# A hybrid attention and convolution step: four convolution inputs as filling of the attention, and two gates by Strassen's product

## The chip, the cores and the metric

The kernel runs on one core of one Trainium2 chip. The metric is the device time of one execution in microseconds. A core has a matrix engine (PE, with its weight loads shown as PEld), a vector engine (DVE), a scalar engine (ACT), a general engine (POOL) and queues that issue transfers (SP's above all). Matrix products go to PSUM, eight banks of 512 float32 columns for each of 128 partitions; everything else lives in SBUF.

## What is computed

One step of an encoder for 1024 frames of a new stream and 32 frames of a running one (TT = 1056 columns in all, D = 1024 channels). Cut to what matters:

```python
h = rmsnorm(x, norm_g)
q, k = rmsnorm(h @ Wq) / 8, rmsnorm(h @ Wk)       # per head of 64, 16 heads
v, logf = h @ Wv, log_sigmoid(h @ Wf + b_f)
ga, gb, ma, mb = h @ Wga, h @ Wgb, h @ Wma, h @ Wmb
u = (h @ Wua) * sigmoid(h @ Wub)                  # the conv input
o = softmax(q k^T + C[t] - C[s], causal) v        # C = cumsum(logf)
conv = causal depthwise conv of u, width 31
ya = (o * silu(ga)) @ w_pa
yb = (silu(layernorm(conv)) * silu(gb)) @ w_pb
y = x + (sigmoid(ma) * ya + sigmoid(mb) * yb) @ w_out
```

Outputs are y, k, v, logf and the last 30 rows of u.

## The kernel before

Data stand with channels on partitions. The normed input is held as two tiles, xh (rounded to the fast matmul type) and xl (the remainder), 8 channel tiles (kt) by 1056 columns each. Each weight block of 1024 x 128 is loaded as raw, split into wh (ACT, `split_w`, L91) and wl (POOL, L94), and a product is wh·xh + wl·xh + wh·xl: three matmuls for each kt.

`steps` (L144) projects one block of 128 output channels: three column ranges of 352, each with 8 kt, so 24 steps of three matmuls (L102). After each step `beat` (L118) is called. It runs what was put off with `later` for that count of beats, adds `pace["rate"]` to a credit, and while the credit is not negative it takes small work for DVE from two lists, `chores` and `taps`, and subtracts its cost (1.0 for a tap, 0.1 for the first tap of a tile, which ACT does).

`taps` holds the depthwise convolution: for each of 8 channel tiles 31 taps (`conv_taps`, L254; L264 is one multiply-add over 1086 columns on DVE), then two entries of `sums` (L251) that add the result to the mean and the sum of squares for the layernorm. A tile's taps enter when both of its projections "ub" and "ua" are done (`u_done`, L292). `u_tile` pumps taps beyond 66 at once; `pump` ignores the credit.

The order is: input and first tile u0; u1, values, u2, values, u3; k and q for eight pairs of heads with u4, u5, u6 between; u7; eight "ga" gates with Silu on ACT; the attention; two last gates; then the projections "pa", "pb" and "out". Up to the attention the orders of PE, DVE and ACT are the program's own (`manual_schedule`); from there on only PE's is, and a scheduler places the others.

The attention (L997 on) walks 132 items: 16 heads of 8 query blocks, and 4 items for the running stream. A block's scores go to PSUM (L938), DVE takes the maximum (L943), ACT the exponential (L946), POOL scales (L949), PE transposes (L966), ACT and DVE split the result (L970, L971), PE multiplies by the values (L982, L983). Scores are started three items ahead. After each item four steps of `filler` run: 22 gates of gb, ma and mb (`gate_steps`, L765), evacuated by ACT from one PSUM bank (pool pq) and stored in scratch. The layernorm's statistics also run there. In the head's last part, DVE multiplies the output with Silu(ga) (L993).

Behind it `a_half` (L1110) splits the attention's output for "pa"; `ln_out` (L1119) makes the other branch's input during "pa"; `outproj` (L1147) runs each projection, its first block with kt outermost.

Of the kernel before, what the change touches and what calls it, by code (L numbers as in the profile page):

```python
# [8 lines left out]
F32 = mybir.dt.float32  # L9
# [19 lines left out]
LNO = ((0,), (1, 2), (3,), (4, 5), (6,), (7,), ())  # L29
LNEXP = "natural_log_exp_and_others"  # L30
NFILL = 22
R_U, R_V, R_QK, R_G, R_A = 0.25, 0.17, 0.19, 0.27, 0.12
# [16 lines left out]
def build(tc, xT, xt, wv, wf, ckT, cv, clT, stT, vec, cst, yT, kT, vO, lfO, cpT, csT):  # L49
# [26 lines left out]
    rawp = [wp]  # L76

# [10 lines left out]
    def split_w(raw, offset=2000):  # L88
        with tc.high_priority(offset=offset):
            wh = wp.tile([128, KT, 128], F32R, name="wh", tag="wh")  # L90
            nc.scalar.copy(wh, raw)  # L91
            wl = wp.tile([128, KT, 128], F32R, name="wl", tag="wl")
            for k0, k1 in WSP:
                nc.gpsimd.tensor_sub(wl[:, k0:k1, :], raw[:, k0:k1, :], f32(wh[:, k0:k1, :]))  # L94
        return wh, wl
# [40 lines left out]
    def fetch():  # L136

        if plan:
            key = plan.pop(0)
            if not plan:  # L140
                rawp[:] = [wp]
# [28 lines left out]
    sg = pool("sg")  # L170

    def t352(name, bufs):
        return sg.tile([128, CH], F32, name=name, tag=name, bufs=bufs)

    pq = pool("pq", 1, space=PS)
    pps = ExitStack()
    pjA = pool("pjA", 4, stack=pps, space=PS)
# [15 lines left out]
    cvp = pool("cvp", 2, stack=pcv)  # L193
    us = {}
    taps = []
    cvt = [cvp]
# [57 lines left out]
    def conv_taps(f):  # L254
        u = us.pop(f)

        def tap(i):
            w = vec_t[:, V_WDW + f * KC + i:V_WDW + f * KC + i + 1]
            if i == 0:
                y = sides["y", f] = cvt[0].tile([128, CW], F32, name="y", tag="y")  # L260
# [4 lines left out]
            if f == 7:  # L265
                tc.keep_in_program_order(t)
# [3 lines left out]
        items = [lambda i=i: tap(i) for i in range(KC)]  # L270
        if f == 7:
            taps.extend(pend + items)
            pend.clear()
        else:
            taps.extend(items[:4] + pend + items[4:])
            pend[:] = sums(f) if f else []
# [7 lines left out]
    def u_tile(f):  # L284
        if f > 2:
            pump(len(taps) - 66)
        u = us[f] = cvt[0].tile([128, UW], F32, name="u", tag="u", bufs=3 if f < 7 else 1)
# [10 lines left out]
    def u_steps(f, pj):  # L298
# [13 lines left out]
        for g, ev in (("ub", ev_ub), ("ua", ev_ua)):  # L312
# [172 lines left out]
    for f in range(8):  # L485
        if f in (2, 4, 6):
            plan.extend([("ub", 3 + f // 2), ("ua", 3 + f // 2)])
        plan.extend([("k", f), ("q", f)])
    plan.extend([("ub", 7), ("ua", 7)] + [("ga", f) for f in range(8)] + [("gb", 0)])
# [24 lines left out]
    rxs = [pool(f"rx{i}", 1, stack=prw) for i in range(2)]  # L514
    rawp.extend(rxs)
# [3 lines left out]
    p2 = ExitStack()  # L519
    u7p = pool("u7p", 1, stack=p2, side="right")  # L520
    pv = ExitStack()
    zp = pool("zp", 1, stack=pv, side="right")
# [4 lines left out]
    xsm = vp.tile([128, KT, TS], F32, name="xsm", bufs=1)  # L527
    nc.vector.tensor_add(xsm, f32(xh[:, :, T:]), f32(xl[:, :, T:]))

    def split_v(c):  # L530
        wh2, wl2, raws2 = [], [], []
        for hf in range(2):
            with tc.high_priority(offset=1500):
                raw = vp.tile([128, 4, VC], F32, name="vraw", tag="vraw", bufs=2)
                nc.sync.dma_start(raw, wv[c, :, hf * 4:hf * 4 + 4, :])
                wh = vp.tile([128, 4, VC], F32R, name="vwh", tag="vwh", bufs=4)
                nc.scalar.copy(wh, raw)
                wl = vp.tile([128, 4, VC], F32R, name="vwl", tag="vwl", bufs=4)
# [15 lines left out]
        def gathered(ps):  # L554
            v4 = vp.tile([TS, 4, VC], F32, name="v4", tag="v4", bufs=1)
            for j in range(4):
                nc.scalar.copy(v4[:, j, :], ps[32 * j:32 * j + 32, :VC])
            vs = vp.tile([TS, VC], F32, name="vs", tag="vs", bufs=1)
# [53 lines left out]
    fp = pool("fp", 1, stack=pv, side="right")  # L612
    NZ = 9 * H
    zf = z.rearrange("p a b -> p (a b)")

    def small(name):
        return fp.tile([128, NZ], F32, name=name, tag=name)

    lf = fp.tile([128, 9, H], F32, name="lf")
    lfs = lf, lf.rearrange("p a b -> p (a b)")  # L620

    def log_sigmoid():
        lf, lff = lfs
        az, ee, s2, ac = small("az"), small("ee"), small("s2"), small("ac")
# [21 lines left out]
    def forget_sums():  # L646

        lfT = fp.tile([H, TT], F32, name="lfT")
# [14 lines left out]
    def forget_rows(lfT):  # L663
        on16 = fp.tile([H, T], F32R, name="on16")
        nc.gpsimd.memset(f32(on16), 1.0)
        ls = fp.tile([H, SKEYS], F32, name="ls")
        nc.sync.dma_start(ls[:, :PAST], clT)
        cc = fp.tile([H, T], F32, name="cc")
        csm = fp.tile([H, SKEYS], F32, name="csm")
# [619 lines left out]
```

## Time and profile before

| | us |
|---|---|
| median of 3 runs | 1394.23 (1394.11 to 1394.41) |
| span of the profiled execution | 1392.1 |
| the median stands above that span by | 2.1 |
| instructions | 24733 |
| bytes moved | 201.24 MB, 145 GB/s |

The page gives each engine's busy time, a strip of 40 slices of the span with the busy share in tenths, the chain of waits followed back from the end, and groups of like instructions by line: "line engine operation out<-in shape xcount | busy us, mean ns of one | idle before it, and what ended that". A matmul's mean ns runs from its start to its modelled end and overlaps the next one's; intervals come from the chain, where a row is "start us, length us, what". Windows give busy time by engine in a stretch.

### The profile page before, as it was taken

Reading aid. Unit: us, or ns where it says so; the run is one execution under the profiler, and the core shown is the slowest. Engines: PE = TensorE matmul, PEld = TensorE weight load, DVE = VectorE, ACT = ScalarE, POOL = GpSimd, SP = SyncE. Lnnn points to the kernel's source line nnn. Section 1 sums busy time; section 2 is a strip of 40 time slices with the busy share of each in tenths; the row PEclk is TensorE's granted clock in tenths of the full one; section 3 lists DMA queues with packets and bytes.
Section 4 is the critical chain, followed back from the end, with each engine's and each line's share of the span. In section 5 each row is a group of like instructions: output and inputs, shape, how many; then the busy total and the mean of one; then the engine's idle time right before and its main releaser. Section 6 shows DMA issues by size and latency. Waiting matters only on the chain.

```text
span 1392.1 us, 24733 instructions
## 1 busy us (share of the span) xinstructions
PE 1384.3 (99%) x9382; PEld 1346.1 (97%) x9382; DVE 906.5 (65%) x1280; ACT 642.7 (46%) x1318; POOL 623.2 (45%) x669
## 2 busy tenths in 40 slices
PE   8999999999999999999999999999999999999999
PEld 7999999999999999999999999999999999999998
DVE  6687787888898999657766767655555487132111
ACT  6333434646464642245555556655555556222100
POOL 2324254657575875443333444343433257254320
PEclk9999999999999999999999999999999999999999
DMA  5253442424342374344545556454642779444431
GB/s 182 93 179 116 153 136 97 155 85 144 98 164 88 124 207 141 116 124 123 144 137 169 155 147 175 118 152 124 174 134 86 266 265 289 135 150 141 143 107 47
DMA packets 110615, 201.24 MB, mean 145 GB/s; under 512 B 17377, under 2 KB 74593, under 8 KB 110497
## 3 DMA queue, kind: packets, MB, share of 16 engines
q1 hardware_dynamic: 110352, 199.60, 45.7%
q8 instruction: 74, 1.21, 0.4%
q14 instruction: 45, 0.36, 0.1%
q10 hardware_dynamic: 144, 0.07, 0.0%
HBM read 129.78 MB, written 69.84 MB: 143 GB/s over the span
## 4 chain that ended last, share of the span: by engine, by line
PE 97%; DVE 1%; ACT 1%; DMA 0%; issue 0%; POOL 0%; SPq 0%; DVEq 0%; POOLq 0%; ACTq 0%
PE pj L102 71%; PE pjv L592 7%; PE ptr L966 5%; PE po L982 3%; PE po L983 3%; PE psS L938 3%; PE psS L939 2%; PE psS L941 1%; PE pst L716 1%; PE pst L715 1%; PE ptx L434 0%; DMA xtok<-xt 0%; ACT xh L436 0%; PE pjs L549 0%; DVE xl L437 0%
## 5 line engine op out<-in xcount | busy, mean ns | idle before, releaser
L102 PE MATMUL pj<-xh,wh 128*128 128x352 f32 (+2 forms) x1536 | 509.3, 332 | 0.4 <-ACT t L771 0.3
L102 PE MATMUL pj<-xl,wh 128*128 128x352 f32 (+2 forms) x1536 | 494.9, 322 | 0.2 <-DVE xl L437 0.2
L102 PE MATMUL pj<-xh,wl 128*128 128x352 f32 (+2 forms) x1536 | 493.2, 321 | 0.0
L94 POOL TENSOR_TENSOR wl<-raw,wh 128x384 fp32r<-128x384 f32 (+1 forms) x258 | 318.6, 1262 | 234.9 <-ACT wh L91 209.6
L264 DVE SCALAR_TENSOR_TENSOR y<-u,vec_t,y 128x1086 f32<-128x1086 f32 x240 | 378.3, 1577 | 11.5 <-ACT y L261 8.2
L102 PEld LDWEIGHTS pj<-xh,wh 128*128 128x128 f32 x1536 | 289.0, 188 | 3.4 <-issue 0.8
L102 PEld LDWEIGHTS pj<-xl,wh 128*128 128x128 f32 x1536 | 288.7, 188 | 1.4 <-DVE xl L437 1.2
L102 PEld LDWEIGHTS pj<-xh,wl 128*128 128x128 f32 x1536 | 289.4, 188 | 0.2 <-DVE wl L456 0.2
L949 POOL TENSOR_SCALAR P<-P,nm 128x128 f32<-128x128 f32 (+7 forms) x128 | 99.0, 773 | 230.6 <-DVE nm L948 203.1
L943 DVE TENSOR_REDUCE nm<-psS 128x1 f32<-128x128 f32 (+7 forms) x128 | 96.4, 754 | 71.9 <-PE psS L941 70.5
L91 ACT CAST wh<-raw 128x1024 fp32r<-128x1024 f32 x86 | 90.1, 1048 | 112.2 <-PE pj L102 81.0
L970 ACT CAST pth<-ptr 128x512 fp32r<-128x512 f32 (+1 forms) x192 | 89.1, 481 | 81.2 <-PE ptr L966 80.9
L971 DVE TENSOR_TENSOR ptl<-ptr,pth 128x512 fp32r<-128x512 f32 (+1 forms) x192 | 103.3, 550 | 24.0 <-ACT pth L970 22.3
L946 ACT ACTIVATE P<-psS,nm 128x128 f32<-128x128 f32 (+7 forms) x128 | 95.3, 744 | 35.0 <-DVE nm L943 30.3
L733 POOL TENSOR_TENSOR ql<-qn,qh 128x352 fp32r<-128x352 f32 (+1 forms) x48 | 64.6, 1346 | 69.2 <-ACT qh L732 49.8
L966 PE MATMUL ptr<-ident,P 128*128 128x128 f32 x576 | 85.0, 275 | 0.0
L982 PE MATMUL po<-pth,V 128*128 128x256 f32 x320 | 79.0, 283 | 0.0
L983 PE MATMUL po<-ptl,V 128*128 128x256 f32 x320 | 78.6, 281 | 0.0
L592 PE MATMUL pjv<-vwh,xh 128*128 128x260 f32 x256 | 72.5, 283 | 0.0
L592 PE MATMUL pjv<-vwl,xh 128*128 128x260 f32 x256 | 72.5, 283 | 0.0
L592 PE MATMUL pjv<-vwh,xl 128*128 128x260 f32 x256 | 72.3, 283 | 0.0
L938 PE MATMUL psS<-KB,QB 128*128 128x256 f32 (+2 forms) x192 | 67.9, 355 | 0.0
(213 smaller groups left out, 2460.8 us busy)
## 6 DMA issues: line engine op xcount, KB each, us to landing
raw<-wf SPq DMA_DIRECT2D x88, 512.0 KB
s_v<-vb SPq DMA_DIRECT2D x32, 256.0 KB
QB<-s_q SPq DMA_DIRECT2D x32, 256.0 KB
KB<-s_k SPq DMA_DIRECT2D x32, 256.0 KB
V<-s_v SPq DMA_DIRECT2D x16, 512.0 KB
kT<-qn SPq DMA_DIRECT2D x8, 528.0 KB
s_ga<-t SPq DMA_DIRECT2D x24, 176.0 KB
s_gb<-t SPq DMA_DIRECT2D x24, 176.0 KB
```

The source lines that it names most:

```text
L94: nc.gpsimd.tensor_sub(wl[:, k0:k1, :], raw[:, k0:k1, :], f32(wh[:, k0:k1, :]))
L102: nc.tensor.matmul(ps, a[:, kt, :], b(kt, sl), start=(first and n == 0), stop=(last and n == N - 1))
L264: t = nc.vector.scalar_tensor_tensor(y, u[:, i:i + CW], w, y, op0=ALU.mult, op1=ALU.add)
L592: nc.tensor.matmul(ps[:, :VC], a, b, start=(n == 0), stop=(n == 23))
L938: nc.tensor.matmul(ps[:, b, :wm], QB[:, qsl], KB[:, ksl], start=True, stop=False)
L943: nc.vector.tensor_reduce(nm[:, 0:1], ps[:, :nb, :w], axis=AX.XY, op=ALU.max, negate=True)
L946: nc.scalar.activation(P[:, :nk].rearrange("p (b w) -> p b w", b=nb), ps[:, :nb, :w], AF.Exp, bias=nm[:, 0:1], accum_out=nm[:, 1:2])
L949: nc.gpsimd.tensor_scalar(P[:, :nk], P[:, :nk], nm[:, 2:3], 1.0, op0=ALU.mult, op1=ALU.mult)
L966: nc.tensor.transpose(pt[:, 128 * j:128 * j + 128], P[:, 128 * (4 * u + j):128 * (4 * u + j) + 128], ident)
L971: nc.vector.tensor_sub(ptl[:, js, qo], p3, f32(pth[:, js, qo]))
L982: nc.tensor.matmul(po[:, :256], V[:, j, :], pth[:, j, :], start=(j == 0), stop=False)
L983: nc.tensor.matmul(po[:, :256], V[:, j, :], ptl[:, j, :], start=False, stop=(j == njb - 1))
```

## The change

Four conv inputs (u4 to u7) are no longer projected between k and q; they are steps of the attention's filling, in `FILLS`, with seven ga gates and six ma gates. In them the sigmoid is written with a tanh, and one ACT table with exp and tanh is loaded ahead of the attention: ACT writes tanh from PSUM, DVE forms (tanh + 1)·ua from PSUM, ACT halves it. ga is stored without Silu; Silu and the multiplication move into `a_half`. The layernorm's statistics move behind the Strassen stage, to the second block of "pa" (`LNO` is shifted by one block).

After the attention two ma gates run while DVE, ACT and POOL form combinations of x (`xf`, from halves of the columns, 528 wide, and halves of the channels); then gb and mb run as eight pairs of output blocks. Each pair does seven half-size products, in the Winograd form of Strassen's scheme, instead of eight: products of 2 column halves of 264 and 4 kt, with weight combinations made by DVE (`sa`, `sb`) and split by ACT and POOL. Four PSUM accumulators of two banks (tags a to d) take them. The stage has its orders on PE, DVE and ACT written out again. At the head of the last pair all taps left are pumped. Pools move between the two sides of SBUF.

```diff
-R_U, R_V, R_QK, R_G, R_A = 0.25, 0.17, 0.19, 0.27, 0.12
+R_U, R_V, R_QK, R_S, R_A = 0.25, 0.17, 0.19, 0.17, 0.12
+HT = TT // 2
+HC = HT // 2
+SPAIRS = [(g, 2 * i) for g in ("gb", "mb") for i in range(4)]
+FILLS = [("u", 4), ("ga", 1), ("ga", 2), ("ga", 3), ("u", 5), ("ga", 4), ("ga", 5), ("ga", 6), ("u", 6), ("ga", 7),
+         ("ma", 0), ("ma", 1), ("u", 7), ("ma", 2), ("ma", 3), ("ma", 4), ("ma", 5)]
...
+        def tanh_ua(c, sl, ps):
+            for a, b in pieces(c * CH, CH):
+                nc.vector.scalar_tensor_tensor(u[:, b], u[:, b], 1.0, ps[:, a], op0=ALU.add, op1=ALU.mult)
...
     def filler():
-        for n in range(NFILL):
-            yield from gate_steps(*fills.pop(0), pq)
+        for g, f in FILLS:
+            if g == "u":
+                yield from u_steps(f, pq)
+            else:
+                yield from gate_steps(g, f, pq)
...
+    def form_sums(j, fourth):
+        b12, b22 = part[j]
+        b11 = x32(nc.vector, j, 0)
+        nc.vector.tensor_sub(b11, b12, b11)
+        high_of(1, j, b11)
+        nc.vector.tensor_sub(b22, b22, b11)
+        high_of(2, j, b22)
...
+        def made(self, i):
+            if i == 0:
+                self.w = [None] * 4
+                self.split(0, self.r0)
+            elif i == 1:
+                self.sa = srp.tile([128, KT, 128], F32, name="sa", tag="sa")
+                nc.vector.tensor_add(self.sa[:, 4:, :], self.r1[:, :4, :], self.r1[:, 4:, :])
+                nc.vector.tensor_sub(self.sa[:, :4, :], self.sa[:, 4:, :], self.r0[:, :4, :])
+                pace["credit"] -= 0.9
...
+        def product(self, i):
+            tag, wi, half, mov = PRODUCTS[i]
+            if i < 4:
+                self.ps[tag] = ps4.tile([128, 2, 512], F32, name="ps4", tag=tag)
+            ps = self.ps[tag]
+            wh, wl = self.w[wi]
+            for c in range(2):
+                for kt in range(4):
+                    h, l = mov(kt, c)
+                    k = 4 * half + kt
+                    for n, (a, x) in enumerate(((wh, h), (wl, h), (wh, l))):
+                        nc.tensor.matmul(ps[:, c, :HC], a[:, k, :], x, start=(i < 4 and kt == 0 and n == 0),
+                                         stop=(kt == 3 and n == 2), skip_group_check=(i >= 4))
+                    beat()
+                    yield
+            later(2, lambda: self.evac(i, ps[:, :, :HC]))
...
+    PRODUCTS = (("a", 0, 0, part_of(0, 0)), ("b", 1, 0, form(2)), ("c", 1, 1, form(1)), ("d", 2, 0, part_of(0, 1)),
+                ("a", 0, 1, part_of(4, 0)), ("c", 2, 1, part_of(4, 1)), ("d", 3, 0, form(0)))
...
     for n, b in enumerate(seq):
...
-            fill(4 if b.i > 2 or b.head.h != 8 else 0)
+            fill(4)
...
+    pace["credit"] = -9.0
...
+    later(44, lambda: third_sums((0, 1), nc.gpsimd))
+    for f in (6, 7):
+        for _ in gate_steps("ma", f, pjB):
+            pass
...
+    pace["rate"] = R_S
+    for k, p in enumerate(pairs):
+        nxt = pairs[k + 1] if k + 1 < len(pairs) else None
+        later(2, lambda: p.made(5))
+        if k == 0:
+            pace["credit"] -= 8.0
+            later(1, lambda: third_form((0, 1)))
+            later(3, lambda: (third_low((0, 1)), third_sums((2, 3), nc.vector)))
+            later(8, lambda: third_form((2, 3)))
+            later(10, lambda: third_low((2, 3)))
...
+        for i in range(7):
+            if nxt:
...
+            elif i == 0:
+                pump(len(taps))
+                pcv.close()
+                pap = ExitStack()
+                bg = pool("bg", 5, stack=pap, side="right")
+            elif i in (3, 4):
+                later(2, lambda i=i: (a_half(2 * i - 6), a_half(2 * i - 5)))
+            for _ in p.product(i):
+                pass
```

In the part left out, `evac` takes each product from PSUM: ACT copies the first (and the fifth, to scratch); DVE adds the others to it, and charges a credit of 0.43 for each of five. `third_form` overwrites half of xh by a combination that product 3 ("d") reads; `third_low` does the same for xl.

More of the change, by code (lines that the diff above doesn't have):

```diff
@@ L76, in build @@
     rawp = [wp]
+    wslot = [0, 1]
     def f32(ap):
@@ L1046, in build, with x32, high_of @@
-    ones_f = cp.tile([128, 128], F32, name="ones_f", tag="ob")
-    nc.vector.memset(ones_f, 1.0)
-    ln = layernorm()
-    sides["shift"] = ap.tile([128, TT], F32, name="shift", bufs=1)
-    nc.sync.dma_start(sides["shift"], s_m)
+    def x32(eng, kt, hf):
+        t, sl = t528(), slice(hf * HT, hf * HT + HT)
+        eng.tensor_add(t, f32(xh[:, kt, sl]), f32(xl[:, kt, sl]))
+        return t
+    xf = []
+    part = {}
+    def high_of(i, j, t):
+        nc.scalar.copy(xf[i][:, 0, j, :], t)
@@ new lines, in build, with first_pair @@
+    xf.extend(ar.tile([128, 2, 4, HT], F32R, name="xf", tag=f"s{i}") for i in range(3))
+    pairs = []
+    pace["credit"] = -9.0
+    def first_pair():
+        pairs.extend(Pair(k) for k in range(len(SPAIRS)))
+        pairs[0].load()
+    form_adds(0)
+    for j in range(4):
+        later(9 * j + 2, lambda j=j: form_sums(j, j < 2))
+        if j < 3:
+            later(9 * j + 4, lambda j=j: form_adds(j + 1))
+        later(9 * j + 7, lambda j=j: form_lows(j))
+    later(13, first_pair)
+    for i, at in enumerate((25, 29, 31, 38, 40)):
+        later(at, lambda i=i: pairs[0].made(i))
```

434 lines of the change are left out of this document (273 added, 161 removed).

## The prediction

> **What bounds the kernel now.** I read the page first, then who PE waited for, then the chain of waits, and then single groups and windows for prices.
>
> ```profile
> span 1392.1 us, 24733 instructions
> ...
> PE 1384.3 (99%) x9382; PEld 1346.1 (97%) x9382; DVE 906.5 (65%) x1280; ACT 642.7 (46%) x1318; POOL 623.2 (45%) x669
> ...
> PE   8999999999999999999999999999999999999999
> ...
> DVE  6687787888898999657766767655555487132111
> ...
> PEclk9999999999999999999999999999999999999999
> ```
>
> ```profile
> PE ptx L434 <- DVE xl L437: 1.8, 2, 1.5
> ...
> PE pj L102 <- DVE xl L437: 0.2, 1, 0.2
> ```
>
> PE is busy in every slice at full clock, and the first of the six entries in its list of waits is 1.8 us, the last 0.2, in the whole run. So the time is the number of matmuls times the interval at which they pass, plus whatever stalls a change brings in. DVE is the next engine: eight or nine tenths in the first third, five to seven in the attention, almost idle at the end. The interval is read from the chain, since a matmul's own "mean ns" overlaps its neighbours:
>
> ```profile
> 86.40 32.62 PE pjv L592 x270
> ...
> 223.60 3.82 PE pj L102 x24
> 227.75 3.82 PE pj L102 x24
> ...
> 1086.95 301.71 PE pj L102 x1872
> ```
>
> ```profile
> L592 PEld LDWEIGHTS pjv<-vwh,xh 128*128 128x128 f32 x256 | 48.3, 188 | 0.8 <-issue 0.8
> ```
>
> A matmul of 352 columns takes 3.82/24 = 0.159 us, one of 260 columns 32.62/270 = 0.121 us, each with a weight load of its own in its shadow. On the line between the two, 264 columns take 0.1225 us.
>
> **A. Strassen: -18.7 us.** For two output tiles the gate steps issue 2 x 72 matmuls of 352 columns: 144 x 0.159 = 22.9 us. A pair issues 7 products x 2 halves x 4 kt x 3 = 168 matmuls of 264 columns: 168 x 0.1225 = 20.6 us. That is 2.34 us less, in eight pairs 18.7. No other part of PE's work changes in number: the "u", "ga" and "ma" steps only change places, and the six layernorm matmuls move behind the Strassen stage. The 260-column row bounds this term well: with 0.121 it would be -21, and with a 264-column matmul at 0.126 it would be -14.
>
> **B. The last head without filling: +4 us.** The list FILLS holds 4 x 48 + 13 x 24 = 504 steps. The loop asks for 12 + 132 x 4 = 540. The last nine blocks therefore run bare.
>
> ```profile
> 1081.71 1.92 PE pj L102 x12
> ```
>
> ```profile
> 600.00:850.00 250.00, 249.71 (x1827) 234.96 (x1826) 171.85 (x329) 140.16 (x329) 101.60 (x170) 1.00 0.51 143
> 850.00:1080.00 230.00, 229.99 (x1687) 215.89 (x1686) 132.93 (x302) 131.47 (x311) 83.93 (x155) 1.00 0.48 137
> ...
> 1053.00:1087.00 34.00, 33.99 (x274) 32.20 (x273) 15.67 (x33) 17.09 (x40) 9.07 (x17) 1.00 0.22 74
> ```
>
> (Columns: stretch, length, then busy us of PE, PEld, DVE, ACT, POOL.) The last head took 34 us, of which nine fills of 1.92 us are 17.3. PE has 16.7 us left there, beside 15.7 of DVE and 17.1 of ACT (of these some 3 belong to the filling). Throughput is just even, so what is lost is latency in the loop scores, maximum, exponential, transposes: between 0 and half of the bare time (8). I take 4, nearer to the even throughputs.
>
> **C. The forms before product 3: +17 us.** While "ma" 6 and 7 run (48 steps, 22.9 us) and products 0 to 2 of the first pair (24 steps of 3 x 0.1225, 8.8 us), DVE and POOL must make the combinations of x. Product 3 needs the last of them about 33 us after the attention's end. Counted from the diff up to there: POOL has 14 additions of 528 columns, 7 subtractions of 512 for the weights of the pair, and 1,024 columns for "ma" 7, in all 12,000 columns; DVE has 40 operations of 528 (or 512) columns, both inputs in SBUF.
>
> ```profile
> L94 POOL TENSOR_TENSOR wl<-raw,wh 128x384 fp32r<-128x384 f32 x12 | 12.0, 1018 | 53.1 <-ACT wh L91 53.1
> ```
>
> ```profile
> L94 POOL TENSOR_TENSOR wl<-raw,wh 128x384 fp32r<-128x384 f32 x66 | 102.1, 1567 | 44.2 <-ACT wh L91 44.2
> ```
>
> ```profile
> L1115 DVE TENSOR_TENSOR al<-a,ah 128x1056 fp32r<-128x1056 f32 x8 | 10.8, 1357 | 6.2 <-ACT ah L1114 6.2
> ```
>
> The first row is from 1300 to 1392 us, with DVE idle: 2.65 ns a column. The second is from 200 to 600 us, beside a dense DVE: 4.08. The same operation becomes half as slow again when both read SBUF. POOL alone would need 12,000 x 2.65 = 32 us, which just fits (stall 1 with the last casts). Beside a dense DVE it needs 49 (stall 49 + 2 - 33 = 18). One after the other, with DVE's 40 x 528 x 1.285 = 27 us, it would be 59 (stall 28). I take 17, since DVE is dense here, with ends 1 and 28. The Trainium skill ("SBUF — State Buffer", section "Who interferes with whom") states an exclusive lock: a DVE instruction with two SBUF inputs and a GpSimd instruction that reads SBUF run strictly in turn; taken at its word the sum would be the last of the three, +28.
>
> **D. The taps left in the queue: +57 us, and +2 for the clock.** This decides the sign. DVE's convolution taps wait in a queue, and each step of PE work (a beat) gives credit for a share of a tap. Up to the gate "ga" 0 all is drained: four tiles are there and about 480 beats. The other four tiles now enter in the attention, 31 taps each, with ten entries of sums: 134. They leave at R_A = 0.12 a beat.
>
> ```profile
> 680.00:820.00 140.00, 82.28 (x456) 72.20 (x456) 1.00 0.53 149
> ```
>
> ```profile
> 680.00:820.00 140.00, 24.82 (x19) 1.00 0.53 149
> ```
>
> The first row counts PE's projection matmuls in that stretch of the attention, 456, so 152 beats; the second the taps, 19 (0.12 x 152 = 18). So the pace written in the code is what the chip does. In the new attention 456 beats pass with a tap in the queue: 55, and with the cheap first taps 56 entries leave, so 78 stay. "ma" 6 and 7 start from a credit of -9 and end at -5; the first pair takes another 8 off; no tap leaves. Each later pair earns 56 x 0.17 = 9.5 and pays 5 x 0.43 + 2 x 0.9 = 3.95, which leaves 5.6 taps: in pairs 1 to 6, less the debt of 7, some 28 entries. At the head of the last pair stand 50: 45 taps on DVE, one on ACT, four sums. There the change pumps them all at once, in a stage where DVE runs in program order, ahead of the evacuation of the pair before (bank "d") and of all of the last pair.
>
> ```profile
> L264 DVE SCALAR_TENSOR_TENSOR y<-u,vec_t,y 128x1086 f32<-128x1086 f32 x19 | 25.5, 1341 | 0.0
> ```
>
> ```profile
> L264 DVE SCALAR_TENSOR_TENSOR y<-u,vec_t,y 128x1086 f32<-128x1086 f32 x147 | 240.8, 1639 | 8.0 <-ACT y L261 5.8
> ...
> L234 DVE TENSOR_TENSOR y<-y,shift 128x1024 f32<-128x1024 f32 x5 | 7.0, 1408 | 4.3 <-DMA s_y<-y 4.3
> L241 DVE TENSOR_TENSOR mean<-mean,y 128x1024 f32<-128x1024 f32 x5 | 6.4, 1277 | 0.0
> ```
>
> ```profile
> L971 DVE TENSOR_TENSOR ptl<-ptr,pth 128x512 fp32r<-128x512 f32 x94 | 64.4, 687 | 21.4 <-ACT pth L970 20.0 <-issue 0.4
> ```
>
> POOL has little to do then, so I price a tap at 1.341: 45 x 1.341 = 60.3, the two sums 2 x (1.41 + 1.28 + 0.6 for their short pieces) = 6.6, together 67 us. DVE comes to it five beats (1.8 us) before the last pair begins, is through at 65.2, and evacuates bank "d" (0.7, as for 512 columns of PSUM) at 65.9. Product 3 writes that bank, 24 beats or 8.8 us into the pair. PE stands still for 65.9 - 8.8 = 57 us. Lower end 50 (fewer entries, shorter waits), upper end 70 (taps at 1639).
>
> After so long a stop the clock may have fallen back. No row shows PE stopped later than its start; there the warm-up matmuls of 256 columns read:
>
> ```profile
> 1.50:5.50 4.00, 4.00 (x19) 4.00 (x20) 1.00 0.93 311
> 5.80:8.60 2.80, 2.80 (x26) 2.80 (x25) 1.00 1.04 413
> ```
>
> 19 in 4.0 us, then 26 in 2.8: half the pace for about 4 us, though the page prints the granted clock as full. A restart like it costs some 2 us, none if the clock stays; I take 2. The Trainium skill ("TensorE: Matmul & The Clock Gate", section "HAM oscillation — how this bites in real kernels") holds that an idle stretch beyond some 3.4 us lets the array fall back to half rate.
>
> **E. The attention's output halves: +6 us.** The eight a_half were made beside two gates; now each carries a multiplication too, four come inside the last pair behind the queue, four after it. One costs DVE 1.6 (as the next row), 1.36 (L1115) and 0.3.
>
> ```profile
> L1124 DVE TENSOR_TENSOR y<-y,rstd 128x1056 f32<-128x1056 f32 x8 | 12.9, 1618 | 0.1
> ```
>
> From 65.9 us DVE needs 4 x 3.25 + 3.5 for evacuations, to 82.4, then 4 x 3.25, to 95.4. PE ends product 6 at 65.9 + 11.8 + 2 = 79.7 and wants the last half 10 us later: late by 6. Lower end 0, upper 12.
>
> **F. The rest: +4 us.** The u steps in the attention hand one PSUM bank through DVE instead of ACT, 12 times (0 to 6, I take 2). The layernorm, some 11 us of DVE, moves beside the projection "pa" with E's last four:
>
> ```profile
> 1110.00:1200.00 90.00, 90.00 (x557) 90.00 (x556) 58.86 (x49) 48.10 (x57) 51.64 (x29) 1.00 0.79 260
> ```
>
> 59 + 11 + 13 = 83 of 90: still covered, 1 for its tail (0 to 8). In a pair DVE has taps 7.5, weight sums 4 x 0.75 and evacuations 5 x 0.7, 14 of 20.6 us; 1 for lateness (0 to 8). The multiplication and the table changes that leave the attention were not on PE's path: 0.
>
> **Sum.** -18.7 + 4 + 17 + 57 + 2 + 6 + 4 = +71.3. Against the profiled execution, 1392.1 + 71.3 = 1463.4; the median of the runs before is 2.1 above its span, so 1465.
>
> **Rivals.**
> - *The queue is empty by the last pair.* D goes and E falls to 3. It decides from seven entries: the slack is 8.8 + 1.8 - 0.7 us, or seven taps of 1.341. For it speaks that DVE is idle for 30 to 40% of the attention; against it that the beats, not the idle time, release taps, and 19 in 140 us is just that rate. With C at its lower end: 1394.2 - 18.7 + 4 + 1 + 3 + 4 = 1387; with C at 17, 1403. So only with both is it not slower.
> - *Evacuations pass the queue*, if the order written on DVE doesn't hold. Then the last pair runs on, but the layernorm needs the last sums, and DVE has 67 + 16 of the pair + 26 of a_half + 11 + 59 = 179 us before "pb" can end its first tile, PE 20.6 + 91.8 + 10 = 122: the stall of 57 only moves there: 1394.2 - 18.7 + 4 + 17 + 57 + 4 = 1458.
> - *The lock binds fully*: C at 28 and each of seven pairs late by 1 more: 1465 + 11 + 7 = 1483.
>
> **How the numbers follow.** Mine 0.76, own range 1440 to 1485 (D and C moving by their ends, partly against each other); the empty queue 0.07, of which 0.05 faster and 0.02 slower; evacuations first 0.08; the lock 0.09. The range 1432 to 1490 holds all but the empty queue and the tails. What a measurement can tell from no change is 0.2%, 2.8 us: faster 0.05, same 0.02, slower 0.93.
>
> **What would show it.** Right: one gap of PE of 50 to 60 us in the last pair, ended by a DVE evacuation, with some 45 taps of 1.34 us in a row under it; gaps of some 17 us in all around the first pair, ended by POOL or by DVE after POOL; 168 matmuls in 20.6 us between. Wrong: taps that end before the last pair, no long gap there, or a pair of more than 21 us without a named wait.

## The result and the profile after

The changed kernel takes 1508.75 us (median of 4 runs, 1506.32 to 1510.4), the kernel before on the same chip 1394.17 (1393.94 to 1394.41): a ratio of 1.0821, interval 1.0806 to 1.0836. The forecast was 1465, range 1432 to 1490. The sign, the deciding mechanism and the saving were right; the time is 44 us above the forecast and 19 above the range. The span of the profiled execution grew from 1392.1 to 1508.6, by 116.5 where the sum had 71.3.

The page of the kernel after, its first part and three of its strips:

```profile
span 1508.6 us, 25287 instructions
...
PE 1386.0 (92%) x9574; PEld 1339.5 (89%) x9574; DVE 996.0 (66%) x1348; ACT 653.5 (43%) x1310; POOL 652.6 (43%) x694
...
PE   8999999999999999999999996699970489999999
...
DVE  6788788887726666767666676848999677433211
...
PEclk9999999999999999999999998799995689999999
```

PE's strip now has three dents: slices 25 and 26 (905 to 980 us, the end of the last head, the two "ma" gates and the first pair), 30 to 32 (1094 to 1207, the last pair and the start of "pa") and a small one behind. In the two large ones the granted clock falls too. Slices 27 to 29, the Strassen pairs between, are full.

Who PE waited for, in the whole run after ("engine line <- releaser: us in total, times, longest"):

```profile
PE ps L1117 <- DVE t L1145: 65.3, 1, 65.3
PE pj L109 <- ACT t L765: 14.4, 3, 10.0
PE pj L109 <- POOL wl L101: 8.0, 5, 3.7
PE pj L109 <- ACT wh L98: 6.6, 2, 4.5
PE ps L1117 <- ACT xh L1173: 5.4, 1, 5.4
PE ps L1117 <- ACT t L765: 3.3, 1, 3.3
PE ps L1117 <- DVE t L1141: 3.0, 1, 3.0
PE pst L726 <- ACT sqh L716: 2.9, 1, 2.9
```

Before, the largest of these was 1.8. One entry is more than all the others together; the next ones are evacuations and weights that come from ACT and POOL.

Windows after (stretch, length, busy us and count of PE, PEld, DVE, ACT, POOL, then granted clock, DMA share and GB/s):

```profile
900.00:1000.00 100.00, 72.90 (x479) 69.42 (x479) 69.26 (x79) 31.75 (x55) 54.76 (x42) 0.86 0.19 64
1000.00:1100.00 100.00, 100.00 (x824) 100.00 (x823) 80.35 (x70) 25.56 (x31) 63.48 (x37) 1.00 0.33 113
...
1120.00:1186.00 66.00, 0.97 (x8) 0.76 (x7) 61.92 (x50) 1.56 (x2) 3.58 (x2) 0.53 0.04 16
1186.40:1190.40 4.00, 4.00 (x19) 4.00 (x20) 1.50 (x3) 1.45 (x4) 3.60 (x3) 0.50 0.85 299
1190.40:1194.40 4.00, 4.00 (x27) 4.00 (x27) 1.26 (x1) 2.62 (x3) 0.23 (x1) 0.75 1.01 358
```

Between the dents Strassen's product runs without a stop: 824 matmuls in 100 us, 0.1214 us each (0.1225 was assumed). In the 66 us of the third row PE issues 8 matmuls while DVE is busy for 61.9, at a clock of 0.53. After it PE passes 19 matmuls in 4 us, then 27, where 4.00/0.1214 = 33 is the full pace: 20 lost, 2.4 us.

The whole difference can be added up from the starts of the matmuls. If each distance between two neighbours is split into the usual (median) distance of its kind and the rest, the usual distances sum to 1359.9 us before and 1340.9 after (-19.0), the distances over 0.6 us add 118.3 beyond it, and the smaller lengthenings, most of them at a clock below 1, add 17.3: together 116.5. (In the table below the long distances are given whole, with the usual distance that lies in each; so its rows add up to some 120, about 4 too many.)

| place | forecast | measured after |
|---|---|---|
| A, Strassen | -18.7 | -19.0 |
| qk stage | 0 | 4.1, some 3 by the clock |
| B, the last head | +4 | +1.6 |
| C, "ma" gates and first pair | +17 | 19.7 + 9.4 in gaps, some 7 by the clock |
| D, queue of taps | +57 and +2 | 65.6 and 2.8 by the clock |
| last pair's product 6 | in F, 1 | +3.3 |
| E, start of "pa" | +6 | 9.3, 3.7 by the clock |
| later in "pa" | in F, 1 | 7.0, 2.9 by the clock |

### The profile page after: what moved, and what is told of

Same layout as the page of the kernel before. It is cut to its first block, busy times and chain, and to the rows that moved or that the text cites. A ratio compares the mean times of both kernels' runs of the same rounds, so it can differ in the third digit from the quotient of the medians.

```text
span 1508.6 us, 25287 instructions
## 1 busy us (share of the span) xinstructions
PE 1386.0 (92%) x9574; PEld 1339.5 (89%) x9574; DVE 996.0 (66%) x1348; ACT 653.5 (43%) x1310; POOL 652.6 (43%) x694
## 4 chain that ended last, share of the span: by engine, by line
PE 79%; DVE 10%; DMA 4%; issue 3%; ACT 2%; POOL 1%; SPq 0%; DVEq 0%; POOLq 0%; ACTq 0%
PE pj L109 48%; PE ps L1117 9%; PE pjv L607 6%; DVE y L273 4%; PE ptr L971 4%; PE po L987 3%; PE po L988 2%; PE psS L943 2%; PE psS L944 2%; DMA s_ya<-sma 1%; DMA s_k<-qh 1%; POOL wl L101 1%; DVE t L1015 1%; PE psS L946 1%; DVE y L1358 1%
## 5 line engine op out<-in xcount | busy, mean ns | idle before, releaser
L109 PE MATMUL pj<-xh,wh 128*128 128x352 f32 (+3 forms) x1152 | 387.0, 336 | 14.9 <-ACT t L765 14.4
L109 PE MATMUL pj<-xl,wh 128*128 128x352 f32 (+3 forms) x1152 | 373.2, 324 | 0.2 <-DVE xl L455 0.2
L109 PE MATMUL pj<-xh,wl 128*128 128x352 f32 (+3 forms) x1152 | 372.2, 323 | 0.1
L101 POOL TENSOR_TENSOR wl<-raw,wh 128x384 fp32r<-128x384 f32 (+1 forms) x210 | 242.5, 1183 | 193.8 <-ACT wh L98 171.9
L109 PEld LDWEIGHTS pj<-xl,wh 128*128 128x128 f32 x1152 | 217.8, 189 | 1.4 <-DVE xl L455 1.4
L109 PE MATMUL pj<-ah,wh 128*128 128x352 f32 x768 | 187.8, 327 | 6.6 <-ACT wh L98 6.6
L1117 PE MATMUL ps<-xh,wh 128*128 128x264 f32 x256 | 76.7, 300 | 74.0 <-DVE t L1145 65.3
L109 PEld LDWEIGHTS pj<-ah,wh 128*128 128x128 f32 x768 | 136.1, 192 | 7.3 <-ACT wh L98 7.2
L109 PE MATMUL pj<-ah,wl 128*128 128x352 f32 x384 | 125.7, 327 | 8.1 <-POOL wl L101 8.0
L98 ACT CAST wh<-raw 128x1024 fp32r<-128x1024 f32 x70 | 73.4, 1048 | 93.2 <-PE pj L109 85.4
L744 POOL TENSOR_TENSOR ql<-qn,qh 128x352 fp32r<-128x352 f32 (+1 forms) x48 | 56.6, 1179 | 72.4 <-ACT qh L743 56.4
L109 PEld LDWEIGHTS pj<-ah,wl 128*128 128x128 f32 x384 | 73.8, 192 | 10.0 <-POOL wl L101 9.9
```

The costliest lines, as they stand in the source:

```text
L109: nc.tensor.matmul(ps, a[:, kt, :], b(kt, sl), start=(first and n == 0), stop=(last and n == N - 1))
L1117: nc.tensor.matmul(ps[:, c, :HC], a[:, k, :], x, start=(i < 4 and kt == 0 and n == 0), stop=(kt == 3 and n == 2), skip_group_check=(i >= 4))
```

## The experiments

The column "over before" is the time less that of the kernel before on the same chip. The change and e11 are medians of four runs, the others one run each. The four runs of the change spread over 4.1 us, so differences of 2 or 3 us between rows say little by themselves.

| run | us | before, same chip | over before |
|---|---|---|---|
| the change | 1508.75 | 1394.17 | 114.6 |
| e1_drop | 1451.89 | 1395.65 | 56.2 |
| e2_pace | 1442.02 | 1395.65 | 46.4 |
| e3_banks | 1501.97 | 1395.65 | 106.3 |
| e4_dve_adds | 1502.73 | 1395.65 | 107.1 |
| e5_plain | 1438.48 | 1395.2 | 43.3 |
| e6_combo | 1430.52 | 1395.2 | 35.3 |
| e7_cover | 1418.17 | 1395.2 | 23.0 |
| e8_load | 1443.07 | 1395.2 | 47.9 |
| e9_pa_early | 1411.49 | 1394.41 | 17.1 |
| e10_swap | 1413.69 | 1394.41 | 19.3 |
| e11_halves | 1411.31 | 1394.68 | 16.6 |

### The queue of taps: taken out, then drained earlier

The timeline of DVE after, around the long gap (start, length, instruction, count, and idle time before it):

```profile
1109.29 0.70 DVE L1145 TENSOR_TENSOR t<-pu,ps 128x528 f32<-128x528 f32 x1 [2.13 <-PE ps L1117]
1109.91 16.09 DVE L273 SCALAR_TENSOR_TENSOR y<-u,vec_t,y 128x1086 f32<-128x1086 f32 x10
...
1178.85 1.35 DVE L273 SCALAR_TENSOR_TENSOR y<-u,vec_t,y 128x1086 f32<-128x1086 f32 x1
1182.93 1.33 DVE L243 TENSOR_TENSOR y<-y,shift 128x1024 f32<-128x1024 f32 x2 [2.73 <-DMA s_y<-y]
1184.19 1.33 DVE L250 TENSOR_TENSOR mean<-mean,y 128x1024 f32<-128x1024 f32 x2
1185.43 0.70 DVE L1145 TENSOR_TENSOR t<-pu,ps 128x528 f32<-128x528 f32 x1
```

The queue runs from 1109.91 to 1185.43, 75.5 us with 46 taps of DVE, and the evacuation at 1185.43 is the one that PE waits for. It began 10.8 us before PE's gap, as forecast (1.8 + 8.8). Two experiments ask whether the gap is the queue's and nothing else's. The first leaves its middle taps out (`middle` is every tap of a tile but its first and last), so a part of the convolution isn't computed:

```diff
-                pump(len(taps))
+                taps[:] = [t for t in taps if t not in middle]
+                pump(len(taps))
```

> Leaves out 43 of the 45 DVE taps that are pumped at the head of the last pair (all but each tile's last), so part of the convolution is not computed; everything else stands. My theory (the pumped queue holds up the evacuation of bank d): of the 75 us that DVE spends there some 43 x 1.385 = 60 go, the gap of PE before product 3 of the last pair shrinks from 65 us to about 6, the cold clock behind it goes, and the time is 1508.7 - 60 - 3 = 1446 (1438 to 1452). The rival (the lost time only moves, to the attention's halves or to the layernorm, since DVE is busy there anyway): over 1475.

Measured: 58.3 us less (relative to before on the same chip). The 43 taps left out, at a step of 1.385 (1.35 and 0.04 between), make 59.6. What is left of the wait in that kernel, from 1000 to 1210 us:

```profile
PE ps L1119 <- DVE t L1147: 5.7, 1, 5.7
```

So PE's gap was set by these taps, one for one. The second keeps all the work and lets taps leave faster in the attention:

```diff
-R_U, R_V, R_QK, R_S, R_A = 0.25, 0.17, 0.19, 0.17, 0.12
+R_U, R_V, R_QK, R_S, R_A = 0.25, 0.17, 0.19, 0.17, 0.22
```

> All work kept; the attention's pace is raised from 0.12 to 0.22 tap a beat, and by the code's own credit the queue is empty in pair 6, so nothing is pumped. My theory: DVE in the attention rises from some 67% to 82% and still keeps up; the 65 us gap, 3 of cold clock, 3 behind it and some 4 of the attention's halves go: 1433 (1425 to 1442). The rival (DVE in the attention has no room, since taps stand in the way of maxima and evacuations): PE gaps of 20 us or more in the attention, 1455 or above.

Measured: 68.2 us less, nine short of what was expected. The gap of 65.3 is gone and little took its place in the attention, where DVE had the room (busy for 360 of the 475 us from 430 to 905, instead of 311): two new distances of some 1.6 us are all that shows there. So D isn't a price of the change itself but of a pace left at 0.12. What was missed is what remains, 46 us, where the forecast without D and its clock would have left 12.

### The forms: the port, or the evacuations behind them

The timeline of DVE after, at the end of the attention:

```profile
920.20 0.71 DVE L1015 TENSOR_TENSOR t<-xh,xl 128x528 f32<-128x528 f32 x1
924.61 1.79 DVE L1033 TENSOR_TENSOR t<-t 128x528 f32<-128x528 f32 x1 [3.70 <-POOL t L1015]
...
936.40 1.83 DVE L1015 TENSOR_TENSOR t<-xh,xl 128x528 f32<-128x528 f32 x1
938.27 1.70 DVE L1040 TENSOR_TENSOR t<-t 128x528 f32<-128x528 f32 x1
...
974.51 2.27 DVE L1177 TENSOR_TENSOR xl<-t,xh 128x528 fp32r<-128x528 f32 x2
```

The timeline of POOL and that of ACT, same stretch:

```profile
923.28 6.02 POOL L1015 TENSOR_TENSOR t<-xh,xl 128x528 f32<-128x528 f32 x4 [16.10 <-DMA s_o<-ot]
...
935.88 3.52 POOL L1015 TENSOR_TENSOR t<-xh,xl 128x528 f32<-128x528 f32 x2
```

```profile
930.65 0.63 ACT L1022 CAST xf<-t 128x528 fp32r<-128x528 f32 x1 [1.86 <-DVE t L1040]
931.18 1.04 ACT L98 CAST wh<-raw 128x1024 fp32r<-128x1024 f32 x1
932.13 0.44 ACT L765 COPY t<-pj 128x352 f32<-128x352 f32 x1
```

Two things are to be seen. The same kind of addition takes DVE 0.71 alone and 1.7 to 1.8 while POOL adds; POOL passes one in 3.52/2 = 1.76 then, and DVE one in the same time, in turns. That is the price which the forecast bounded from both sides. The Trainium skill ("SBUF — State Buffer", "Who interferes with whom") has the two running strictly in turn; these rows agree, with one limit: POOL's first two additions at 923.28 took 1.3 each, so that one of each would need 2.0 strictly in turn, and they pass in 1.76. But POOL isn't full: 54.8 busy of 100 us, and its first addition waits until 923.28 for a DMA. And the copy of the gate's PSUM bank (L765) stands on ACT behind casts that wait for DVE, which waits for POOL. PE stops 10.0 us for it, since three banks are all that the gates have. The forecast knew the first and not the second. Two theories can be held: the forms are done when DVE and POOL have taken their turns, and PE's stops only show that (the port); or the gates' evacuations behind the forms are a loss of their own. Two edits were to tell them apart: six banks for the gates, or all additions of POOL on DVE, which ends most of the turns (POOL still splits the weights).

```diff
-    pjB = pool("pjB", 3, stack=pB, space=PS)
+    pjB = pool("pjB", 6, stack=pB, space=PS)
```

> One size: the pool that takes the results of the two ma gates behind the attention has 6 banks instead of 3, so PE can run both gates without an evacuation. Theory port (DVE and POOL take turns at SBUF, and the forms are done when they are done): the 18 us of gaps inside the two gates go, but the products of the first pair wait longer by about as much; total changes by less than 5: 1504 to 1512. Theory evacuation (ACT's written order holds the gates' results behind the forms, and that wait is a loss of its own): 1491 (1486 to 1496).

```diff
-        eng.tensor_add(t, f32(xh[:, kt, sl]), f32(xl[:, kt, sl]))
+        nc.vector.tensor_add(t, f32(xh[:, kt, sl]), f32(xl[:, kt, sl]))
...
-        nc.gpsimd.tensor_add(t2, f32(xf[2][:, 0, j, :]), f32(xf[2][:, 1, j, :]))
+        nc.vector.tensor_add(t2, f32(xf[2][:, 0, j, :]), f32(xf[2][:, 1, j, :]))
```

> The additions of the forms move from POOL to DVE (16 of 528 columns), the rest stands. Theory port: an addition costs POOL 1.3 alone and 1.8 beside DVE, and stretches DVE's own operation from 0.7 to 1.8; on DVE it costs 0.7. DVE's stretch from 920 to 977 us falls by 7 to 10 us, and so does the time: 1500 (1496 to 1503). The rival (DVE is simply the longest of the three engines there, so more work on it lengthens the stretch by 16 x 0.7 = 11): 1515 or above.

The banks give 8.3 us, the additions 7.5. The first lies between the two predictions, so the time settles for neither; the traces do. Waits from 900 to 990 us, first with six banks, then with the additions on DVE:

```profile
PE ps L1117 <- ACT t L765: 5.8, 1, 5.8
PE ps L1117 <- ACT xh L1173: 5.3, 1, 5.3
PE pj L109 <- ACT wh L98: 2.7, 1, 2.7
```

```profile
PE pj L109 <- ACT t L765: 10.0, 3, 7.4
PE ps L1117 <- ACT t L765: 4.3, 1, 4.3
PE ps L1117 <- ACT xh L1173: 4.0, 1, 4.0
```

Six banks take the gates' own waits for copies away, 14.4 us; the same copies then hold up product 1 of the first pair for 5.8, and the wait for xh stays. Behind them the forms run as before. Their first addition on POOL and their last write of xl on DVE, with six banks:

```profile
916.54 6.17 POOL L1015 TENSOR_TENSOR t<-xh,xl 128x528 f32<-128x528 f32 x4 [10.21 <-DMA s_o<-ot]
...
967.78 2.27 DVE L1177 TENSOR_TENSOR xl<-t,xh 128x528 fp32r<-128x528 f32 x2
```

Both come 6.7 us earlier than in the changed kernel (923.28 and 974.51), and what lies between is as long as it was. So the evacuations were no loss of their own. The whole chain starts earlier, since the attention's last matmul starts at 911.1 us instead of 919.0: with three banks, 51 matmuls of the gate "ma" 6 (8.1 us) had run inside the last head and put its end off; with six they wait until the head is through, and lie over the forms instead.

With the additions on DVE the stretch itself changes. Its first and last rows:

```profile
921.75 1.95 DVE L1015 TENSOR_TENSOR t<-xh,xl 128x528 f32<-128x528 f32 x3 [3.06 <-DMA s_o<-ot]
...
965.22 1.33 DVE L1177 TENSOR_TENSOR xl<-t,xh 128x528 fp32r<-128x528 f32 x2
```

From the first addition of the forms to the last write of xl that is 44.8 us, against 56.6 in the changed kernel and 57.8 with six banks, although DVE does 14 operations more in it. So the turns, and DVE's waits for POOL's results (8.7 us in the changed kernel), cost at least 12 us. A part of that is lost again, because DVE now waits for the DMA that POOL waited for. It is one chain, DVE with POOL, then ACT, with PE behind it at whichever place comes first.

### Strassen undone, with the taps drained

The 18 gates run plainly behind the attention, with seven banks and no forms; the pace of e2 is kept, and holds in these gates too, which start without the debt of 9.

```diff
-    pjB = pool("pjB", 3, stack=pB, space=PS)
...
-    pace["credit"] = -9.0
...
+    pjB = pool("pjB", 7, stack=pB, space=PS)
+    pace["rate"] = 0.22
...
+    for g, f in [("ma", 6), ("ma", 7)] + [(g, f) for g in ("gb", "mb") for f in range(8)]:
...
+        for _ in gate_steps(g, f, pjB):
```

> Strassen undone alone: the four conv inputs stay in the attention (pace 0.22), the two ma gates and then gb and mb run as 18 plain gates behind it, without forms, and four of the attention's halves are made beside the last two. Theory stalls (the forms before product 3, the tight start of pa and the cold clock behind their gaps cost the Strassen stage more than its 19 us): against the 1442 of the same pace with Strassen it gains 30 of gaps and 7 of clock there and some 8 at the start of pa, and pays 19: 1416 (1408 to 1422). Rival (moving the conv inputs into the attention is what costs): 1435 or above.

A miss: 1438.48, only 3 us under e2 (43.3 over before against 46.4). But the edit did something else besides. The waits from 890 to 940 us, led by

```profile
PE ptr L971 <- DVE ptl L976: 5.3, 3, 2.6
PE psS L943 <- ACT P L951: 4.1, 2, 3.0
```

are 13.3 us in the last head's own steps, and some 8 more go there by a lower clock. That isn't the price of a head without filling. With six banks (e3) and in the combination below (e6) the last head has no filling and no gate in it either, and takes half the time. Windows of that stretch, first e3, then this run, and DVE's largest group in this run:

```profile
889.90:911.10 21.20, 19.32 (x179) 16.57 (x178) 14.83 (x33) 13.83 (x34) 6.87 (x15) 1.00 0.11 34
```

```profile
894.70:935.00 40.30, 26.99 (x179) 23.23 (x178) 39.85 (x56) 16.60 (x39) 16.51 (x19) 0.70 0.10 31
```

```profile
L273 DVE SCALAR_TENSOR_TENSOR y<-u,vec_t,y 128x1086 f32<-128x1086 f32 x18 | 27.1, 1508 | 0.2
```

PE's count of matmuls is the same (179). Here DVE is full, with taps that run between the head's steps; in e2, e3 and e6 no tap runs there. Why the taps of the gates come so early isn't shown; in the gates, where they belong, DVE then stands idle from 1000 to 1100 us. So this run doesn't answer its question. As an estimate, with the head at e3's 21 us it would have taken 1438.5 - 19 = some 1419, inside the range of the theory that the Strassen stage, as built, costs more than its 19 us. No run tried that.

### Together, and with cover for the forms

The three edits above (pace, banks, additions) in one kernel:

```diff
-R_U, R_V, R_QK, R_S, R_A = 0.25, 0.17, 0.19, 0.17, 0.12
+R_U, R_V, R_QK, R_S, R_A = 0.25, 0.17, 0.19, 0.17, 0.22
...
-    pjB = pool("pjB", 3, stack=pB, space=PS)
+    pjB = pool("pjB", 6, stack=pB, space=PS)
...
-        eng.tensor_add(t, f32(xh[:, kt, sl]), f32(xl[:, kt, sl]))
+        nc.vector.tensor_add(t, f32(xh[:, kt, sl]), f32(xl[:, kt, sl]))
```

> The pace of 0.22, the six banks and the additions on DVE together. If the three losses are separate: 1442 - 6.7 - 6 = 1429 (1425 to 1433). If banks and additions answer the same loss: 1435 (1433 to 1438).

1430.52: as expected. The gains overlap by some 5 us (68.2 + 8.3 + 7.5 = 84.0, of which 79.3 are seen). Then four gates instead of two stand over the forms, the forms are spread over their beats, and filling is left out at the first three blocks of seven heads, so that the last head has some again:

```diff
-R_U, R_V, R_QK, R_S, R_A = 0.25, 0.17, 0.19, 0.17, 0.12
+R_U, R_V, R_QK, R_S, R_A = 0.25, 0.17, 0.19, 0.20, 0.25
...
-          ("ma", 0), ("ma", 1), ("u", 7), ("ma", 2), ("ma", 3), ("ma", 4), ("ma", 5)]
+          ("ma", 0), ("ma", 1), ("u", 7), ("ma", 2), ("ma", 3)]
...
-            fill(4)
+            fill(4 if b.i > 2 or b.head.h % 2 or b.head.h == 0 else 0)
...
-        later(9 * j + 2, lambda j=j: form_sums(j, j < 2))
+        later(18 * j + 2, lambda j=j: form_sums(j, j < 2))
```

> As the combination, with twice the cover for the forms: ma 4 and 5 leave the filling and run behind the attention too, so four gates (46 us) lie over the forms, whose steps are spread over them; the attention skips 48 steps of filling at the first three blocks of seven heads, where there is little to wait for; paces 0.25 and 0.20 keep the queue empty. Theory (DVE and POOL take turns and need some 45 to 50 us for the forms, so only cover helps): the gaps from the attention's end to product 6 of the first pair fall from some 18 to under 4, 1429 - 15 = 1414 (1409 to 1420). Rival (the chain through ACT's and DVE's written order holds the gates up whatever the cover, or the thinner filling bares the attention): 1425 or above.

1418.17, 12.3 us less. Of C two gaps are left (4.8 and 1.6 us), the first again product 3 waiting for xh (L1173). The forms end no sooner after their first addition (58.3 us), but there is more work over them. ACT's casts of xh wait 7.11 and then 4.42 us for DVE, which has three taps ahead of what the first need and four additions ahead of what the last need.

### The small stops: the qk stage and the start of "pa"

Between k and q the change took three u blocks away; after it, PE stands 3.2 us at 353 us for the squares of q (L716). Loading the first head after that loop, so that its DMAs don't share the queue, was to cure it:

```diff
-        if f == 7:
-            heads[0].load()
...
+    heads[0].load()
```

> Pace 0.22, and the first head's eight loads are issued behind the last key and query projection instead of before the last pair of them. Theory (the loads of 2 MB crowd the stores of q and k, so that ACT waits for a free buffer and PE for ACT): the 3 us gap at 353 us and the slow clock behind it go: 1442 - 6 = 1436 (1433 to 1438). Rival (the first scores now wait for the loads): the gap moves to the attention's start, 1442 or above.

A miss: 1443.07. A gap of 2.75 stayed there. One of 2.63 came in at 403 us, which isn't the rival's either: PE waits for squares on DVE, and DVE had waited 5.65 for the DMA of a finished convolution tile (s_y). In the changed kernel ACT's timeline names what it waits for at 351 us:

```profile
351.22 0.48 ACT L743 CAST qh<-qn 128x352 fp32r<-128x352 f32 x1 [4.42 <-DMA s_k<-qh]
```

The cast needs a buffer that its own store to scratch still reads. Giving the tiles qh and ql a third buffer, in the next run, did take the gap away. That run also moves the split of the first weights of "pa":

```diff
-            qh = tp.tile([128, CH], F32R, name="qh", tag="qh")
-            ql = tp.tile([128, CH], F32R, name="ql", tag="ql")
+            qh = tp.tile([128, CH], F32R, name="qh", tag="qh", bufs=3)
+            ql = tp.tile([128, CH], F32R, name="ql", tag="ql", bufs=3)
...
+            elif i == 2:
+                rawa = load_raw(("pa", 0))
+            elif i == 6:
+                later(1, lambda: split.update({("pa", 0): split_w(rawa)}))
...
-    raw = load_raw(("pa", 0))
-    split["pa", 0] = split_w(raw)
```

> As the version with four gates over the forms, and two moves: the first weights of pa are loaded at product 2 of the last pair and split at its product 6 (their slot is free after product 5), instead of behind everything; the buffers of the rounded q and k are 3 instead of 2. Theory (PE's 6.6 and 4.5 us gaps at the start of pa are the weights' split, queued on ACT and POOL behind the attention's halves, and not the halves): 9 of the 11 us and 2 of cold clock go there, 3 at 353 us: 1418 - 14 = 1404 (1399 to 1409). Rival (the halves themselves are late and take the wait over): 1412 or above.

1411.49: the 6 us of the qk stage and nothing of "pa" (its two gaps are 6.0 and 4.5 us). The ACT timeline of the changed kernel shows the place:

```profile
1202.58 1.07 ACT L1198 CAST ah<-a 128x1056 fp32r<-128x1056 f32 x1 [1.73 <-DVE a L1196]
1203.56 1.08 ACT L1194 ACTIVATE g<-g 128x1056 f32<-128x1056 f32 x1
1205.45 1.08 ACT L1194 ACTIVATE g<-g 128x1056 f32<-128x1056 f32 x1 [0.82 <-DMA g<-s_ga]
1206.44 1.03 ACT L98 CAST wh<-raw 128x1024 fp32r<-128x1024 f32 x1
```

The cast of the weights (L98) stands behind the halves' steps, which wait for their own loads; POOL's half of the split follows it, 0.7 to 2.1 us a piece. It is the weights that PE waits for, not the halves. The next run tried two orders: product 4 before product 3 in the first pair, and a higher priority for the splits of "pa".

```diff
-        for i in range(7):
+        for i in ((0, 1, 2, 4, 3, 5, 6) if k == 0 else range(7)):
...
-        w = split.pop(key) if key in split else split_w(load_raw(key))
+        o = 6000 if key[0] in OUTW else 2000
+        w = split.pop(key) if key in split else split_w(load_raw(key, o), o)
```

> As the run before it, and in the first pair product 4 goes ahead of product 3 (2.9 us more cover for the last combinations of x), and the weights of the three projections at the end are split with a higher priority on ACT and POOL. Theory: the 4.8 us gap at product 3 falls to about 2, and the 1.7 and 3.5 us gaps in the middle of pa go: 6 to 8 us under the run before it. Rival (those gaps are DVE's and POOL's turns at SBUF in pa, which priority doesn't change): 2 to 3 under it.

A miss, 1413.69: the gaps in the middle of "pa" stay (2.3 and 3.5 us), so their cause is open, and product 4 now waits 7.3 us for the copy of product 0 ("pu", L1128). Its ACT timeline:

```profile
948.40 1.25 ACT L1174 CAST xh<-t 128x528 fp32r<-128x528 f32 x2 [4.42 <-DVE t L1173]
949.56 0.59 ACT L1128 COPY pu<-ps 128x528 f32<-128x528 f32 x1
```

The copy was ready to go and stood behind casts that waited 4.42 us for DVE. Last, the halves were cut in three, so that loads and multiplications come early and only casts stay late, with the weights' split written at product 3:

```diff
-    def a_half(f):
+    def a_load(f):
...
+    def a_mul(f):
...
+    def a_cast(f):
...
-                bg = pool("bg", 5, stack=pap, side="right")
+                bg = pool("bg", 6, stack=pap, side="right")
...
+            elif i == 3:
+                later(1, lambda: split.update({("pa", 0): split_w(rawa)}))
+                later(3, lambda: (a_cast(2), a_cast(3), a_load(4), a_load(5)))
```

> The version before this one (weights of pa split at product 6, 1411.5 us) with every a_half cut in three: loads, Silu and multiplication, cast. Loads and multiplications move to products 0 to 5 of the last pair, six buffers instead of five, and only the casts of the last four halves stay behind the last product; the split of pa's first weights stands at product 3, ahead of the chain on ACT. Theory: the two gaps at the start of pa (6.0 and 4.5 us) come from ACT's written order, the weights queued behind halves that wait for their loads; then both fall under 1 us each and the time is 1401 (1398 to 1405). Rival: DVE and the loads of the halves themselves are too slow for pa's first block; then waits for ah of 5 us or more take the place of those for wh and wl, and the time stays above 1406.

A miss for both: 1411.31, no change. Against the kernel before its ratio is 1.012 (interval 1.0103 to 1.0137). The two waits at the start of "pa" are gone; one of 6.0 us for an evacuation (DVE t L1141) stands in their place, in product 6, and smaller ones for an evacuation and for wl in "pa" make up the rest. ACT's timeline in that kernel:

```profile
1102.99 1.04 ACT L98 CAST wh<-raw 128x1024 fp32r<-128x1024 f32 x1 [6.36 <-PE ps L1117]
1103.94 2.04 ACT L1206 CAST ah<-a 128x1056 fp32r<-128x1056 f32 x2
...
1107.85 0.58 ACT L1131 COPY t<-ps 128x528 f32<-128x528 f32 x1
```

The cast waits 6.36 us for PE: the weights of "pa" use a buffer that the last pair's third weights hold until product 5 has run. Behind it on ACT stands the copy of product 4 (L1131), for which DVE's evacuation and so product 6 wait. So the loss at the start of "pa" follows ACT's written order, here with a buffer that comes free late; a version that gives these weights a buffer of their own wasn't tried. No version ran faster than the kernel before.

## Why the prediction was right or wrong

- **What bounds the kernel.** Right: PE's own pace, so that each stall shows in full.
- **A.** Right: -19.0 for -18.7.
- **D.** The mechanism was right in each part (queue, place, the bank waited for, 46 taps for 45), and e1 and e2 show that it is the whole of that gap. The term was undersized by some 9. Of the queue's 75.5 us, 42 taps take 58, at a step of 1.385 instead of 1.341; four taps beside POOL's work take 9.8 (three at the head, and one of 3.4 us while POOL adds to rstd); the sums take 5.0 of the 6.6 that they were priced at, and a wait for a DMA, which had no price, 2.7. The clock's 2 was right (2.4 to 2.8); the windows gave it 0.53 in the gap and 0.50 behind. The rule cited for it (the Trainium skill, "TensorE: Matmul & The Clock Gate", "HAM oscillation — how this bites in real kernels") agrees here.
- **C.** The step that failed. Its way of reckoning, length of the forms less what PE has to do meanwhile, was right; both sides were mis-sized, and the clock was left out. From the attention's end to the last write of xl the forms took 57.8 us, where the forecast had 49 + 2: nearer to its upper end, the price strictly in turn. And PE had only some 25 us of work over them, not 33, because 51 of the gates' matmuls had already run in the last head. That leaves 33, and 2 more go behind it at a lower clock. Seen from PE it is 29.1 us in gaps and some 7 by the clock, for which C had no term: 36 instead of 17, and above the upper end of 28. The gaps end on ACT, not on POOL or DVE as the forecast would have had it; that is the place where PE meets the chain, and e3 shows that it adds nothing to its length.
- **B.** 1.6 instead of 4, with gate matmuls in the last head, which the forecast didn't see. Its reason holds: where the head runs really bare (e3, e6), its 17.1 us of usual distances take 21.2, so 4 are lost (some 1 of that also in the last head before). What the overlap saved here, C paid for with 8 us of cover.
- **E and F.** E's size is not far off (9.3 and 3.7 for 6), its cause was wrong: not a late half but weights whose split stands behind the halves on ACT, as e9 and e11 show. In the middle of "pa", where F had allowed 1, there are 7.0 and 2.9; weights are waited for there too, but the one run aimed at it (e10) changed nothing, so the cause is open. The qk stage, held to be free, took 4.1 and some 3 by the clock; a third buffer gave 6 back. F's lateness of a pair shows only in the last one (3.3).
- **The range.** Four sums went past their upper ends: C, the start of "pa" (13.0 for 12), its middle (9.9 for 8) and the qk stage (7 for 0); D was 9 above its middle. The range had let such ends partly cancel. They share one omission: only D had a term for the clock, and behind the other stops PE lost some 7, 3, 4 and 3 us by it, 17 of the 44 above the forecast. That the queue wasn't empty and that evacuations didn't pass it were read rightly. Of the rival in which the lock binds fully, the 28 in C came close to the 29.1 of gaps; its late pairs did not come.

## What to carry to other kernels

When work moves, ask for every engine whose order is written out what now stands in front of each PSUM evacuation and each weight split; a cast that waits for another engine holds both back, however idle its engine looks (ACT was at 43%). But the place where PE stops need not be the loss: compare the length of the chain behind it in two runs before the place is blamed (56.6 and 57.8 us with three and six banks). Read a control's trace before its time: e5 was meant to take Strassen out, and put taps into the last head as well. A queue released by a pace per step must be counted again when entries are added to it: a constant left at 0.12 put 46 taps into the last pair. And price a stop of PE with the time in which it comes back to its clock.

## What was not expected of the hardware

- A few stops close together cost more clock than one long one: between 900 and 1000 us, with stops of 10.3, 5.8, 3.6 us and less, the mean granted clock is 0.86, and the matmuls lose some 7 us beyond the gaps; behind the stop of 65.6 us they lose 2.8.
- Behind the long stop the page prints 0.50 for the 4 us with 19 matmuls; at the start of the kernel before it had printed 1.00 for the same pace. There the count of matmuls tells more than the printed clock.
